# A forgetting-attention layer on one core: transposing the softmax weights on the tensor engine for part of the keys

## The chip, the core and the metric

The kernel runs on one core of one Trainium2 chip. The metric is device time in microseconds (us): the median of three runs, and beside it one execution that the hardware profiler recorded. Engines are named as in the profile: PE is the tensor engine's matmul side and PEld its weight loads, DVE the vector engine, ACT the scalar engine, POOL GpSimd, SP the engine whose queue issues most transfers.

## The reference

One layer of an encoder trunk with 2048 positions and width 1024. The token mixer is causal attention with 16 heads of 64 and a forgetting bias; a dense squared-ReLU MLP follows.

```python
logits = einsum(q_i, k) * scale + (F_i[..., :, None] - F[..., None, :])   # F = cumsum log sigmoid(f_pre + b_f)
logits = where(k_pos[None, :] <= q_pos[:, None], logits, -inf)
p = softmax(logits)
o = einsum(p, v)                     # per block of 128 queries
x = x + g_m * (o @ w_out)
h = rms_norm(x, norm_mlp) * (1 + sc_f) + sh_f
x = x + g_f * (square(relu(h @ w_mlp_in)) @ w_mlp_out)
```

q, k, v come from a normed and modulated x times `fox_w_in`; q and k are RMS-normed per head.

## The kernel before

The program has two parts. The first (0 to about 1,500 us of the profile) holds the attention, the second the MLP.

**Units.** The 16 heads are worked in 8 groups `g` of two heads `h`, and the queries in 16 blocks `i` of 128. A unit is one block of one head: 256 units, of which 128 have `i` of 8 or more, with 1,152 to 2,048 keys. For each unit

- `att_scores` computes the scores on PE (L537, L538, mask L540) into a PSUM tile `S` of up to 1,024 keys; DVE adds the forgetting row and takes the running maximum (L544), writing the scores to the SBUF tile `L`. L549 makes the negative maximum `st`.
- `att_exp` lets ACT take the exponential of all keys in place (L555), and then write, in pieces of up to 1,024 keys (`PW`), the fp16 high half times 32,768 (`PSCALE`) to a tile `ph` (L562).
- `att_transpose` lets DVE write the low half, `L` times 32,768 minus the high half, behind it into the same `ph` (L574). In group 7, for blocks 8 to 15, POOL does the last 256 keys of a piece in two steps (L578 scales, L579 subtracts). Then SP issues a transposing transfer of high and low halves from `ph` to a tile `pT` (L582).
- `att_values` multiplies on PE: per 128 keys one matmul with the high part (L600) and one with the low part (L601), with `pT` as weights, into `po`.

**Buffers.** `L` has 3 buffers (`NL`), `ph` 4 (`NPH`), `pT` 5 (`NPT`). PSUM has two tiles `S`, one bank `T` (`psT`, one buffer, also used when the normed q and k are transposed on PE in `sweep_norm`, L435 and L445), two banks `Q` for the projections and one for `po`.

**Order.** `attention()` is written so that the values of a unit come about three units after its scores. Between them the `sweeps()` generator puts the projections of the next group (L487 to L489, 24 matmuls for 128 positions, with operands split into high and low parts by ACT L406 and POOL L407). The order on each engine's queue is fixed when the program is built, by a list scheduler that works with its own estimates of durations; on the chip each queue runs in that order and waits on semaphores.

**Second part.** The output projection and the MLP, almost all PE (L132 to L134), weights split by ACT L864 and DVE L865.

Of the kernel before, what the change touches and what calls it, by code (L numbers as in the profile page):

```python
# [6 lines left out]

# [17 lines left out]
P = 128  # L25
# [4 lines left out]
HD = 64  # L30
# [9 lines left out]
PSCALE = 32768.0  # L40
PW = 1024
# [10 lines left out]
QSH, QDM = 0, 0  # L52
LEAD0, NORM_AT, ADA0, ADA1, NF = 0.5, 8, 60, 10, 5
# [4 lines left out]
def fox_layer(ctx, tc, x, c, norm_mix, norm_mlp, w_ada, b_ada, w_mlp_in, w_mlp_out,  # L58
# [116 lines left out]
    with ExitStack() as st:  # L175
# [161 lines left out]
        def value_scale(g):  # L337

            wv = sb.tile([P, KB, P], F32, tag="ph" if g else "k", name=f"wv{g}", bufs=NPH if g else NK)
            nc.sync.dma_start(wv, w_in[:, 2 * D + g * P:2 * D + (g + 1) * P].rearrange("(k p) c -> p k c", p=P))  # L340
            r = sb.tile([P, 2], F32, tag="lsr", name=f"lsr_w{g}", bufs=2)
            nc.scalar.activation(wv, wv, AF.Square, accum_out=r[:, 0:1])
            lw = sb.tile([P, 2], F32, tag="lw", name=f"lw{g}", bufs=2)
            log_sum(r, lw, f"w{g}")
            nc.vector.tensor_tensor(lw, lw, hs2, op=ALU.add)
            nc.scalar.activation(vsc[:, g:g + 1], lw[:, 0:1], AF.Exp, scale=-0.5)
            nc.vector.tensor_scalar(vsc[:, g:g + 1], vsc[:, g:g + 1], PSCALE, None, op0=ALU.mult)
            nc.vector.reciprocal(osc[:, g:g + 1], vsc[:, g:g + 1])
            nc.vector.tensor_scalar(osc[:, g:g + 1], osc[:, g:g + 1], 1.0 / PSCALE, None, op0=ALU.mult)

# [171 lines left out]
        def att_scores(g, i, h, st, L):  # L522
# [6 lines left out]
            for cch in range(j + 1):  # L529
# [11 lines left out]
                if last or cch % 2 == 1:  # L541
                    c0, c1 = cch // 2 * 2 * TJ, cch * TJ + w
                    with pri(PR_T):
                        nc.vector.tensor_tensor_reduce(  # L544
                            out=L[:, c0:c1], in0=s2[:, :c1 - c0], in1=Fb[g, h, cch // 2][:, :c1 - c0],
                            scale=1.0, scalar=-3.0e38, op0=ALU.add, op1=ALU.max, accum_out=mx[:, cch // 2:cch // 2 + 1])
                yield
            with pri(PR_T):
                nc.vector.tensor_reduce(out=st[:, h:h + 1], in_=mx[:, :j // 2 + 1], axis=AX.X, op=ALU.max, negate=True)  # L549

        def att_exp(g, i, h, st, L):
# [6 lines left out]
            for s0 in range(0, W, PW):  # L558
                w = min(PW, W - s0)
                ph = sb.tile([P, 2 * PW], F16, tag="ph", name=f"ph{g}_{i}_{h}_{s0}", bufs=NPH)  # L560
                with pri(PR_E):
                    nc.scalar.activation(ph[:, :w], L[:, s0:s0 + w], AF.Copy, scale=PSCALE)  # L562
# [3 lines left out]
        def att_transpose(g, i, h, L, phs):  # L566
            W = (i + 1) * P
            pts = []
            for n, ph in enumerate(phs):
                s0 = n * PW  # L570
                w = min(PW, W - s0)
                c = w - min(w, POOL_B * P) if i >= POOL_I and g >= POOL_G and w > TJ else w
                with pri(PR_PL):
# [9 lines left out]
                pts.append(pT)  # L583
            return pts
# [4 lines left out]
        def att_values(g, i, h, st, pts):  # L589
# [5 lines left out]
            for b in range(nb):  # L595
                v = vT[g, b // RB][:, b % RB, h, :]
                pT, bb = pts[b * P // PW], b % (PW // P)
                nw = min(PW // P, nb - b + bb)
                with pri(PR_PO):
                    nc.tensor.matmul(po[:, h, :], lhsT=pT[:, bb, :], rhs=v, start=(b == 0), stop=False)  # L600
                    nc.tensor.matmul(po[:, h, 0:HD], lhsT=pT[:, nw + bb, :], rhs=v[:, 0:HD],  # L601
# [345 lines left out]
```

## Time and profile before

| what | us |
|---|---|
| median of 3 runs (3115.86 to 3118.42) | 3117.88 |
| profiled execution, its own time | 3121.49 |
| span of that execution | 3119.8 |
| first part, 0 to 1,500 us: PE busy / DVE busy / ACT busy / POOL busy | 1259.7 / 1232.3 / 977.3 / 747.7 |
| second part, 1,500 to 3,120 us: PE busy | 1610.7 |

An engine's busy time is what its instructions cover. Matmuls are pipelined, so PE counts as busy while a matmul drains that no longer hinders the next one. The clock column is the share of full TensorE clock that was granted. "DMA" is the mean busy share of 16 DMA engines; a little over 1.0 means packets that overlap.

### The profile page before, as it was taken

The numbers are of one execution on the slowest core, as the hardware profiler recorded it, in microseconds if no ns is written. First come the engines' busy times: TensorE is split into PE (matmuls) and PEld (weight loads), VectorE is DVE, ScalarE is ACT, GpSimd is POOL, SyncE is SP. The second block draws the span as 40 slices with busy tenths as digits, with TensorE's granted clock in tenths as the row PEclk, the third lists the DMA queues.
The fourth block names the chain that finished last, engine by engine and source line by source line (L and its number), as shares of the span: only waits on it lengthen the run. The fifth ranks groups of instructions, "written<-read, shape, count | busy, mean of one in ns | idle before, by whom it ended". The sixth has DMA issues, their size and how long they took to land.

```text
span 3119.8 us, 44614 instructions
## 1 busy us (share of the span) xinstructions
PE 2870.4 (92%) x16587; PEld 2375.9 (76%) x16587; DVE 1930.7 (62%) x3319; ACT 1433.1 (46%) x2267; POOL 1040.5 (33%) x811
## 2 busy tenths in 40 slices
PE   4788889888988898988999999999999999999999
PEld 4667777777877777776788888788887888878887
DVE  6688978988888877878356433443335333453334
ACT  4466766666676767766233322232222223222321
POOL 3354545545464645445332100410013001311103
PEclk9799989999999999998999999999999999999999
DMA  8479999999999989979755432543235323352332
GB/s 274 124 174 208 208 193 218 209 204 208 213 209 211 201 191 197 189 163 211 215 191 200 132 93 80 172 138 95 75 108 203 94 81 108 95 192 91 108 94 69
DMA packets 852122, 502.34 MB, mean 161 GB/s; under 512 B 585396, under 2 KB 782076, under 8 KB 851904
## 3 DMA queue, kind: packets, MB, share of 16 engines
q1 hardware_dynamic: 843536, 469.60, 62.1%
q0 software_dynamic: 8368, 29.89, 2.5%
q8 instruction: 130, 2.13, 0.3%
q14 instruction: 88, 0.72, 0.1%
HBM read 310.50 MB, written 46.28 MB: 114 GB/s over the span
## 4 chain that ended last, share of the span: by engine, by line
PE 49%; DVE 1%; DMA 1%; ACT 0%; issue 0%; SPq 0%; POOL 0%; DVEq 0%; ACTq 0%
PE my L134 8%; PE my L132 7%; PE my L133 7%; PE pu L134 7%; PE pu L132 7%; PE pu L133 7%; PE py L132 1%; PE py L133 1%; PE py L134 1%; DVE w L865 1%; DMA w1r<-in_w_mlp_in_dram 1%; PE xt L799 0%; PE e_py L132 0%; DMA pT<-ph 0%; PE e_py L134 0%; PE e_py L133 0%
## 5 line engine op out<-in xcount | busy, mean ns | idle before, releaser
L574 DVE SCALAR_TENSOR_TENSOR ph<-L,ph 128x1024 f16<-128x1024 f32 (+7 forms) x384 | 438.3, 1152 | 81.2 <-ACT ph L562 79.5
L887 POOL TENSOR_TENSOR rl<-rl 128x512 f32<-128x512 f32 x128 | 139.1, 1086 | 1024.6 <-ACT rl L886 1019.7
L864 ACT CAST w<-w1r 128x1024 fp32r<-128x1024 f32 x128 | 133.5, 1043 | 598.6 <-PE my L134 553.5
L132 PE MATMUL my<-w,a 128*128 128x512 f32 x1024 | 405.0, 396 | 0.1
L133 PE MATMUL my<-w,a 128*128 128x512 f32 x1024 | 402.9, 394 | 0.0
L134 PE MATMUL my<-w,a 128*128 128x512 f32 x1024 | 395.9, 396 | 2.9 <-DVE a L890 2.9
L562 ACT ACTIVATE ph<-L 128x1024 f16<-128x1024 f32 (+7 forms) x384 | 301.7, 804 | 177.4 <-DMA pT<-ph 152.6
L407 POOL TENSOR_TENSOR hl<-hl,hh 128x1024 fp32r<-128x1024 f32 x120 | 299.5, 2497 | 243.7 <-ACT hh L406 205.4
L487 PE MATMUL psq<-w,hh 128*128 128x384 f32 (+1 forms) x960 | 343.5, 359 | 26.5 <-DVE v L496 12.5
L489 PE MATMUL psq<-w,hl 128*128 128x384 f32 (+1 forms) x960 | 354.4, 371 | 3.2 <-POOL hl L407 2.9
L544 DVE CUSTOM_DVE_ANT_0 L<-S,F 128x1024 f32<-128x1024 f32 (+7 forms) x384 | 343.1, 904 | 19.5 <-PE S L538 6.7
L488 PE MATMUL psq<-w,hh 128*128 128x384 f32 (+1 forms) x960 | 342.7, 359 | 6.1 <-POOL w L333 6.1
L555 ACT ACTIVATE L<-L,st 128x128 f32<-128x128 f32 (+15 forms) x256 | 306.7, 1198 | 89.2 <-DVE st L549 84.9
L537 PE MATMUL S<-kT,qT 128*128 128x512 f32 (+3 forms) x640 | 261.8, 411 | 77.4 <-DVE mx L544 66.6
L600 PE MATMUL po<-v,pT 128*128 128x128 f16 x2176 | 277.1, 228 | 55.4 <-DMA pT<-ph 47.0
L865 DVE TENSOR_TENSOR w<-w1r,w 128x1024 fp32r<-128x1024 f32 x128 | 169.9, 1328 | 236.6 <-ACT w L864 236.6
L915 DVE TENSOR_TENSOR ya<-my,ya 128x512 f32<-128x512 f32 x192 | 128.0, 687 | 292.7 <-PE my L134 292.7
L134 PE MATMUL pu<-m_h,w 128*128 128x512 f32 x768 | 304.4, 396 | 0.0
L132 PE MATMUL pu<-m_h,w 128*128 128x512 f32 x768 | 303.8, 396 | 0.0
L133 PE MATMUL pu<-m_h,w 128*128 128x512 f32 x768 | 301.8, 393 | 0.0
L865 DVE TENSOR_TENSOR w<-w2r,w 128x1024 fp32r<-128x1024 f32 x128 | 165.7, 1295 | 203.7 <-ACT w L864 203.7
L600 PEld LDWEIGHTS <-pT 128*128 128x128 f16 x2176 | 205.1, 103 | 86.2 <-DMA pT<-ph 58.3
(214 smaller groups left out, 6115.8 us busy)
## 6 DMA issues: line engine op xcount, KB each, us to landing
w1r<-in_w_mlp_in_dram SPq DMA_DIRECT2D x128, 512.0 KB
w2r<-in_w_mlp_out_dram SPq DMA_DIRECT2D x128, 512.0 KB
hl<-hT_d SPq DMA_DIRECT2D x120, 512.0 KB
F<-nF_d SPq DMA_DIRECT2D x64, 256.0 KB
wa<-in_w_ada_dram SPq DMA_DIRECT2D x32, 512.0 KB
x<-in_x_dram SPq DMA_DIRECT2D x27, 512.0 KB
wr<-in_fox_w_in_dram SPq DMA_DIRECT2D x64, 192.0 KB
h_d<-h2r POOLq DMA_DIRECT2D x24, 512.0 KB, 3.4
```

What stands on the lines that cost most here:

```text
L132: nc.tensor.matmul(ps, lhsT=a[0], rhs=b[0], start=first, stop=False)
L133: nc.tensor.matmul(ps, lhsT=a[0], rhs=b[1], start=False, stop=False)
L134: nc.tensor.matmul(ps, lhsT=a[1], rhs=b[0], start=False, stop=last)
L487: nc.tensor.matmul(ps[:, :n], lhsT=hh, rhs=w[:, 0, :n], start=(kb == 0), stop=False)
L488: nc.tensor.matmul(ps[:, :n], lhsT=hh, rhs=w[:, 1, :n], start=False, stop=False)
L489: nc.tensor.matmul(ps[:, :n], lhsT=hl, rhs=w[:, 0, :n], start=False, stop=(kb == KB - 1))
L544: nc.vector.tensor_tensor_reduce(out=L[:, c0:c1], in0=s2[:, :c1 - c0], in1=Fb[g, h, cch // 2][:, :c1 - c0], scale=1.0, scalar=-3.0e38, op0 ...
L555: nc.scalar.activation(L[:, :W], L[:, :W], AF.Exp, bias=st[:, h:h + 1], scale=1.0, accum_out=st[:, 2 + h:3 + h])
L562: nc.scalar.activation(ph[:, :w], L[:, s0:s0 + w], AF.Copy, scale=PSCALE)
L574: nc.vector.scalar_tensor_tensor(ph[:, w:w + c], L[:, s0:s0 + c], PSCALE, ph[:, :c], op0=ALU.mult, op1=ALU.subtract)
L600: nc.tensor.matmul(po[:, h, :], lhsT=pT[:, bb, :], rhs=v, start=(b == 0), stop=False)
L865: nc.vector.tensor_tensor(w[:, 1, :], raw, w[:, 0, :].bitcast(F32), op=ALU.subtract)
```

## The change

For blocks 8 to 15 the weights of a unit are cut differently, by the new function `plan(i)`: keys 0 to 511 are transposed by PE, as fp32, into the PSUM bank `T`; ACT copies them to the high half in a `pT` tile and DVE subtracts to make the low half. Keys 512 to 1,023 form a `ph` piece of their own whose low half POOL makes; keys from 1,024 on stay as they were. Blocks 0 to 7 keep their cut. The factor 32,768 moves into the exponential: `st` is the negative maximum plus ln 32,768, so `L` holds scaled weights; L562 becomes a plain copy, L574 a plain subtraction, the scaling step L578 falls away, and the factor in `osc` too. The maximum is chained from the first score tile to the second instead of reduced at the end.

```diff
+TURN_I, HEADS = 8, ("pe", "pool")
@@ value_scale
-            nc.vector.tensor_scalar(osc[:, g:g + 1], osc[:, g:g + 1], 1.0 / PSCALE, None, op0=ALU.mult)
@@ att_scores
-                            scale=1.0, scalar=-3.0e38, op0=ALU.add, op1=ALU.max, accum_out=mx[:, cch // 2:cch // 2 + 1])
+                            scale=1.0, scalar=mx[:, 0:1] if cch > 1 else -3.0e38, op0=ALU.add, op1=ALU.max, accum_out=mx[:, cch // 2:cch // 2 + 1])
-                nc.vector.tensor_reduce(out=st[:, h:h + 1], in_=mx[:, :j // 2 + 1], axis=AX.X, op=ALU.max, negate=True)
+                nc.vector.tensor_scalar(st[:, h:h + 1], mx[:, j // 2:j // 2 + 1], -1.0, LN_PSCALE, op0=ALU.mult, op1=ALU.add)
+
+        def plan(i):
+            W = (i + 1) * P
+            if i < TURN_I:
+                return [(s0, min(PW, W - s0), "dma") for s0 in range(0, W, PW)]
+            head = [(k * TJ, TJ, how) for k, how in enumerate(HEADS)]
+            return head + [(s0, min(PW, W - s0), "dma") for s0 in range(len(head) * TJ, W, PW)]
@@ att_exp
-            for s0 in range(0, W, PW):
-                w = min(PW, W - s0)
+            for s0, w, how in plan(i):
+                if how == "pe":
+                    phs.append(None)
+                    continue
                 ph = sb.tile([P, 2 * PW], F16, tag="ph", name=f"ph{g}_{i}_{h}_{s0}", bufs=NPH)
-                    nc.scalar.activation(ph[:, :w], L[:, s0:s0 + w], AF.Copy, scale=PSCALE)
+                    nc.scalar.copy(ph[:, :w], L[:, s0:s0 + w])
@@ att_transpose
-                    nc.vector.scalar_tensor_tensor(ph[:, w:w + c], L[:, s0:s0 + c], PSCALE, ph[:, :c],
-                                                   op0=ALU.mult, op1=ALU.subtract)
-                    if c < w:
-                        lt = L[:, s0 + c:s0 + w]
-                        nc.gpsimd.tensor_scalar(lt, lt, PSCALE, None, op0=ALU.mult)
-                        nc.gpsimd.tensor_tensor(ph[:, w + c:2 * w], lt, ph[:, c:w], op=ALU.subtract)
+            for (s0, w, how), ph in zip(plan(i), phs):
+                n = w // P
                 pT = sb.tile([P, 2 * PW // P, P], F16, tag="pT", name=f"pT{g}_{i}_{h}_{s0}", bufs=NPT)
-                with pri(PR_DT):
-                    nc.sync.dma_start_transpose(pT[:, :2 * w // P, :], ph[:, :2 * w])
+                if how == "pe":
+                    pt = psT.tile([P, TJ], F32, tag="T", name=f"pp{g}_{i}_{h}")
+                    for b in range(n):
+                        nc.tensor.transpose(pt[:, blk[b]], L[:, s0 + b * P:s0 + (b + 1) * P], ident)
+                    hi, lo = [pT[:, k * n:(k + 1) * n, :].rearrange("p b c -> p (b c)") for k in range(2)]
+                    nc.scalar.copy(hi, pt)
+                    nc.vector.tensor_tensor(lo, pt, hi, op=ALU.subtract)
+                else:
+                    c = w - min(w, POOL_B * P) if i >= POOL_I and g >= POOL_G and w > TJ else w
+                    c = 0 if how == "pool" else c
+                    with pri(PR_PL):
+                        if c > 0:
+                            nc.vector.tensor_tensor(ph[:, w:w + c], L[:, s0:s0 + c], ph[:, :c], op=ALU.subtract)
+                        if c < w:
+                            nc.gpsimd.tensor_tensor(ph[:, w + c:2 * w], L[:, s0 + c:s0 + w], ph[:, c:w], op=ALU.subtract)
+                    with pri(PR_DT):
+                        nc.sync.dma_start_transpose(pT[:, :2 * w // P, :], ph[:, :2 * w])
```

In the changed kernel L587 is the transposing matmul, L589 ACT's copy, L590 DVE's subtraction, L596 DVE's and L598 POOL's subtraction to `ph`, L600 the transposing transfer, L617 and L618 the values (L600 and L601 before).

The PE queue at the values of group 3, block 11, head 1 (`pT3_11_1_0` is the tile with that unit's first keys; `psq` a projection). Before:

```order
L489 MATMUL psq4_1_2_8982<-w4_4_7897,hl4_6_8871 128x384
L487 MATMUL psq4_1_2_8982<-w4_5_7902,hh4_6_8873 128x384
L488 MATMUL psq4_1_2_8982<-w4_5_7902,hh4_6_8873 128x384
L204 MATMUL pvfg_9116<-ident_129,acc4_7032 128x128
L600 LDWEIGHTS pT3_11_1_0_8945
L600 MATMUL po_192<-v3_0_6138,pT3_11_1_0_8945 128x128
```

And in the changed kernel:

```order
L490 MATMUL psq4_3_1_10522<-w4_7_8291,hh4_13_10323 128x384
L491 MATMUL psq4_3_1_10522<-w4_7_8291,hl4_13_10321 128x384
L587 MATMUL pp3_11_1_9380<-ident_129,L3_11_1_9218 128x128 x4
L617 LDWEIGHTS pT3_11_1_0_9379
L617 MATMUL po_192<-v3_0_6390,pT3_11_1_0_9379 128x128
L204 MATMUL pvfg_9575<-ident_129,acc4_7364 128x128 x8
L587 MATMUL pp3_12_0_9469<-ident_129,L3_12_0_9305 128x128 x4
L618 LDWEIGHTS pT3_11_1_0_9379
```

The four transposes now stand directly ahead of the values that read their result, with ACT's copy and DVE's subtraction in between on their own queues.

The SP queue at blocks 12 and 13 of group 3. The last number pair of a row gives the blocks of 128 columns that a transfer turns (high and low halves together). Before:

```order
L582 DMA_TRANSPOSE pT3_12_0_0_9026<-ph3_12_0_0_8951 128x16x128
L582 DMA_TRANSPOSE pT3_12_0_1024_9029<-ph3_12_0_1024_8953 128x10x128
L582 DMA_TRANSPOSE pT3_12_1_0_9105<-ph3_12_1_0_9032 128x16x128
L582 DMA_TRANSPOSE pT3_12_1_1024_9108<-ph3_12_1_1024_9034 128x10x128
L582 DMA_TRANSPOSE pT3_13_0_0_9198<-ph3_13_0_0_9111 128x16x128
L613 DMA o_d11_83<-ot3_11_9191 128x128
```

And in the changed kernel:

```order
L600 DMA_TRANSPOSE pT3_12_0_512_9476<-ph3_12_0_512_9394 128x8x128
L600 DMA_TRANSPOSE pT3_12_0_1024_9479<-ph3_12_0_1024_9396 128x10x128
L630 DMA o_d11_83<-ot3_11_9650 128x128
L600 DMA_TRANSPOSE pT3_12_1_512_9563<-ph3_12_1_512_9483 128x8x128
L600 DMA_TRANSPOSE pT3_12_1_1024_9566<-ph3_12_1_1024_9485 128x10x128
L600 DMA_TRANSPOSE pT3_13_0_512_9664<-ph3_13_0_512_9570 128x8x128
```

As many transfers stand there as before; the first of each unit turns 8 blocks instead of 16.

## Rows read from the trace of the kernel before

**Rows 1.** Stretches: busy time (instructions) per engine, clock, DMA share, GB/s.
```profile
core 0: us, PE busy (x) PEld busy (x) DVE busy (x) ACT busy (x) POOL busy (x), PEclk, DMA share, GB/s
0.00:1500.00 1500.00, 1259.70 (x9519) 1079.12 (x9520) 1232.27 (x2492) 977.33 (x1657) 747.71 (x568) 0.93 0.94 200
1500.00:3120.00 1620.00, 1610.68 (x7069) 1296.80 (x7067) 698.39 (x827) 455.81 (x610) 292.81 (x243) 1.00 0.38 125
```

**Rows 2.** Stretches of blocks 8 to 15, groups 2 to 7.
```profile
545.00:660.00 115.00, 97.99 (x795) 86.23 (x795) 107.50 (x179) 74.88 (x119) 61.49 (x42) 1.00 0.99 204
...
718.00:837.00 119.00, 104.05 (x787) 87.58 (x785) 104.58 (x174) 81.87 (x127) 65.69 (x44) 0.94 1.03 217
...
885.00:1001.00 116.00, 102.60 (x773) 87.09 (x770) 98.97 (x179) 81.89 (x126) 64.85 (x44) 0.94 1.02 213
...
1054.00:1160.00 106.00, 95.18 (x715) 79.73 (x714) 88.74 (x170) 77.35 (x123) 57.78 (x42) 0.97 0.90 191
...
1217.00:1315.00 98.00, 88.84 (x741) 76.76 (x741) 86.95 (x157) 74.47 (x115) 55.64 (x40) 0.97 0.95 190
...
1382.00:1512.00 130.00, 107.03 (x825) 85.94 (x824) 96.30 (x184) 74.20 (x95) 70.45 (x71) 0.89 0.95 195
```

**Rows 3.** Waits, 0 to 1,500 us: engine, line, releaser; total us, times, longest.
```profile
ACT ph L562 <- DMA pT<-ph: 152.6, 103, 6.4
...
DVE ph L574 <- ACT ph L562: 79.5, 78, 3.6
...
PE S L537 <- DVE mx L544: 66.6, 54, 4.7
...
PE po L600 <- DMA pT<-ph: 47.0, 34, 6.5
...
PE psq L487 <- DVE v L496: 12.5, 7, 4.4
```

**Rows 4.** Groups by shape, 0 to 1,500 us: busy, mean ns; idle before them.
```profile
line engine op names shapes xcount | busy us, mean ns | idle before us <-releasers
...
L574 DVE SCALAR_TENSOR_TENSOR ph<-L,ph 128x1024 f16<-128x1024 f32 x142 | 209.8, 1481 | 36.3 <-ACT ph L562 35.3
...
L562 ACT ACTIVATE ph<-L 128x1024 f16<-128x1024 f32 x160 | 168.1, 1055 | 80.1 <-DMA pT<-ph 76.8 <-DVE acc L197 1.9 <-issue 0.4
...
L448 DVE TENSOR_TENSOR kT<-pqk,kT 64x512 fp32r<-64x512 f32 x64 | 44.1, 689 | 11.3 <-ACT kT L447 9.6
...
L578 POOL TENSOR_SCALAR L<-L 128x256 f32<-128x256 f32 x24 | 30.1, 1258 | 40.6 <-ACT ph L562 37.1 <-issue 3.5
...
L579 POOL TENSOR_TENSOR ph<-L,ph 128x256 f16<-128x256 f32 x24 | 20.7, 863 | 1.1
...
L562 ACT ACTIVATE ph<-L 128x512 f16<-128x512 f32 x32 | 19.8, 623 | 6.4 <-DMA pT<-ph 6.3
...
L445 PEld LDWEIGHTS pqk<-ident,qn 128*128 128x128 f32 x128 | 15.5, 147 | 3.7 <-DVE qT L438 1.8 <-issue 1.5
...
L688 POOL TENSOR_TENSOR e_x<-e_x,wo_raw 128x512 f32<-128x512 f32 x3 | 3.9, 1311 | 2.2 <-DVE wo_raw L687 2.2
...
L668 ACT CAST e_oT<-e_pot 128x512 fp32r<-128x512 f32 x6 | 3.3, 581 | 6.5 <-PE e_pot L667 6.5
```

**Rows 5.** Instructions in order of time near 1,000 us: start, us, what.
```profile
1000.83 1.90 POOL L429 TENSOR_TENSOR qn<-qk,y_q 128x1024 f32<-128x1024 f32 x1 [0.25 <-DVE y_q L127]
...
1001.95 1.86 DVE L574 SCALAR_TENSOR_TENSOR ph<-L,ph 128x1024 f16<-128x1024 f32 x1
...
1008.75 1.22 DVE L574 SCALAR_TENSOR_TENSOR ph<-L,ph 128x1024 f16<-128x1024 f32 x1
```

**Rows 6.** Chain of waits near the attention's end: start, us, what.
```profile
1470.12 6.86 DMA pT<-ph
...
1477.09 1.07 ACT ph L562
...
1478.23 1.62 POOL L L578
1479.86 1.46 SPq L582
...
1481.48 4.79 DMA pT<-ph
```

**Rows 7.** The page's DMA packets, by size.
```profile
DMA packets 852122, 502.34 MB, mean 161 GB/s; under 512 B 585396, under 2 KB 782076, under 8 KB 851904
```

More of the change, by code (lines that the diff above doesn't have):

```diff
@@ L8 @@
+import math
 from contextlib import ExitStack
@@ L40 @@
 PSCALE = 32768.0
+LN_PSCALE = math.log(PSCALE)
 PW = 1024
@@ L566, in att_transpose @@
         def att_transpose(g, i, h, L, phs):
[L567 to L573, printed above, removed]
-                    nc.vector.scalar_tensor_tensor(ph[:, w:w + c], L[:, s0:s0 + c], PSCALE, ph[:, :c],
-                                                   op0=ALU.mult, op1=ALU.subtract)
-                    if c < w:
-                        lt = L[:, s0 + c:s0 + w]
-                        nc.gpsimd.tensor_scalar(lt, lt, PSCALE, None, op0=ALU.mult)
-                        nc.gpsimd.tensor_tensor(ph[:, w + c:2 * w], lt, ph[:, c:w], op=ALU.subtract)
-                pT = sb.tile([P, 2 * PW // P, P], F16, tag="pT", name=f"pT{g}_{i}_{h}_{s0}", bufs=NPT)
-                with pri(PR_DT):
-                    nc.sync.dma_start_transpose(pT[:, :2 * w // P, :], ph[:, :2 * w])
-                pts.append(pT)
@@ L584, in att_transpose @@
-            return pts
+            by_block = []
+            for (s0, w, how), ph in zip(plan(i), phs):
+                n = w // P
+                pT = sb.tile([P, 2 * PW // P, P], F16, tag="pT", name=f"pT{g}_{i}_{h}_{s0}", bufs=NPT)
+                if how == "pe":
[15 more added lines that the diff above has]
+                        nc.sync.dma_start_transpose(pT[:, :2 * w // P, :], ph[:, :2 * w])
+                by_block += [(pT[:, b, :], pT[:, n + b, :]) for b in range(n)]
@@ L586, in fox_layer @@
+            return by_block
         po_of, n_po = {}, [0]
@@ L596, in att_values @@
                 v = vT[g, b // RB][:, b % RB, h, :]
-                pT, bb = pts[b * P // PW], b % (PW // P)
-                nw = min(PW // P, nb - b + bb)
+                p_hi, p_lo = pts[b]
                 with pri(PR_PO):
-                    nc.tensor.matmul(po[:, h, :], lhsT=pT[:, bb, :], rhs=v, start=(b == 0), stop=False)
-                    nc.tensor.matmul(po[:, h, 0:HD], lhsT=pT[:, nw + bb, :], rhs=v[:, 0:HD],
+                    nc.tensor.matmul(po[:, h, :], lhsT=p_hi, rhs=v, start=(b == 0), stop=False)
+                    nc.tensor.matmul(po[:, h, 0:HD], lhsT=p_lo, rhs=v[:, 0:HD],
                                      start=False, stop=(b == nb - 1))
```

## The prediction
> **What bounds the kernel now.** I read the stretches first. After 1,500 us PE is busy 1,610.7 of 1,620 us [rows 1]; the change touches nothing there, so that part keeps its length. All that can move lies in the first 1,500 us, where no engine is full: PE 1,259.7, DVE 1,232.3, ACT 977.3, and the DMA engines at 0.94 [rows 1]. The reader is to see there that PE is idle for 240 us, and that three resources are each close to their limit at once. The changed blocks are read in stretches of their own, from the first scores of block 8 to the first scores of the next group [rows 2]. For groups 2 to 6 these last 115, 119, 116, 106 and 98 us, 554 in all. In them DVE is busy 486.7 us (88%), PE 488.6 us (88%), and the DMA share is 0.90 to 1.03. PEld, the weight loads, whose ends are not modelled as those of the matmuls are, stands at 417.4 us (75%), so PE has more room than its own row says.
>
> Next the waits [rows 3]. PE waits 66.6 us for a score tile that DVE has not yet drained, 47.0 us for a transposed tile, 12.5 us for a projection bank that DVE has not drained. ACT waits 152.6 us for a `ph` tile whose transfer hasn't left, and DVE 79.5 us for ACT behind that. So the transfers hold up ACT, ACT holds up DVE, and DVE holds up PE; but PE pays only 126 us for all three waits named. That is the most that the change can give back on PE, against what it puts on PE.
>
> **The change, part by part.**
>
> PE gets 128 units x 4 = 512 transposes of 128x128 fp32. The same operation stands in the trace: its weight load takes 147 ns [rows 4], which is what a run of them advances by, so 512 x 0.147 = 75 us of PE time, 9.4 us in each group's stretch. No PE work goes away. PE is idle 12% of such a stretch, and as many of the transposes may fall into idle time: **+66 us** (bounds 0, all in idle time, and 75).
>
> New round trips on PE's queue. Values of keys 0 to 511 wait for ACT's copy (0.58 us) and DVE's subtraction (0.69 us) of what PE has just transposed [rows 4]: 1.27 us at least when nothing stands between. In the order on PE's queue 23 of the 128 units have at most 8 matmuls between the last transpose and the first values matmul (15 have none), the other 105 have 23 or more. And bank `T` has one buffer: 14 of the transposes follow those of the unit before by 13 matmuls or fewer, so they wait for the same two steps. (23 + 14) x 1.27 = 47 us if PE had nothing late at those places before; zero if it would have idled there anyway. I take half: **+24 us**. If ACT has an exponential of 2,048 keys ahead of the copy, it is more, and that is in the upper end.
>
> The ring of `pT`. A unit takes three of the five tiles instead of two. Before, the transfer of keys from 1,024 on waits for values of two units earlier; now for the values of keys 0 to 511 of the unit just before (so in the program: the third piece of block 12, head 1, waits for the first piece of block 12, head 0). Release, issue (1.46 us) and landing (4.79 to 6.86 us for 2,048 columns [rows 6]) must now fit into about one unit, and a unit of these blocks lasts 554 us / 80 = 6.9 us. Before they had two. Behind the waiting issue on SP stand the next group's `hl` loads and the output store. On the other side a unit's first transfer turns 1,024 columns instead of 2,048, and over all 128 x 1,024 = 131,072 columns of 256 B leave the DMA queue. The program before turns 557,056 columns, most of the 585,396 packets under 512 B [rows 7], so 24% of them go. Two effects on PE's 47.0 us: down to nothing at best (-47), and at worst a mean wait of 47.0 / 34 = 1.38 us in each of the 128 units (+177 - 47 = +130). The shorter transfer and the tighter ring nearly balance; I take **+10 us**.
>
> DVE loses the 1,024-key subtraction, 1,481 ns [rows 4], and gets one of 512 keys out of PSUM, 689 ns for the nearest row (64 partitions, same length): 128 x 0.79 = 101 us less, 12.7 us per stretch, from 88% to about 77%. The chained maximum and the changed L549 swap one short instruction for another: nothing. What PE can gain from it are the waits on DVE, 66.6 + 12.5 = 79 us; with DVE at 77% I take 70%: **-55 us** (bounds 0 and -79; -101 if DVE alone set the pace).
>
> Of the 1,481 ns part is a collision: at 1001.95 the subtraction took 1.86 us beside a POOL instruction, at 1008.75 it took 1.22 us without one [rows 5]. The new subtraction reads one operand from PSUM, POOL's new one reads two from SBUF. The Trainium skill (SBUF, "Who interferes with whom") says that a vector instruction with two SBUF inputs and a GpSimd instruction that reads SBUF exclude each other, and one with a single SBUF input is free. The two rows agree. By that rule POOL's added time would fall on the subtractions that DVE keeps and give back some 30 of the 101 us; the sum would be about 15 us higher.
>
> POOL gets 128 subtractions of 512 keys. The nearest rows are 863 ns for 256 keys of the same kind and 1,311 ns for 512 of fp32 [rows 4]: 1.3 us each (up to 1.7), 166 us on an engine with 752 us free, less the 30.1 us of L578. It is hidden by that idle time. What loses if the cover goes is the split of the projection's operand queued behind it. ACT does two copies of 512 keys instead of one of 1,024: 2 x 0.62 - 1.06 = 0.19 us x 128 = 24 us, hidden, with 523 us free.
>
> The end of the attention. Group 7 has no projections left to fill with, and its stretch lasts 130 us instead of 111. The chain there runs through a transfer of 6.86 us, L578 with 1.62 us and a transfer of 4.79 us [rows 6]. L578 goes, and the first transfer of each unit halves: **-10 us** (bounds 0 and -19).
>
> Sum: 66 + 24 + 10 - 55 - 10 = **+35 us**. The profiled execution took 3,121.49 us with a span of 3,119.8, 3.6 above the median of 3,117.88; on the median 3,117.9 + 35 = **3,153 us**.
>
> **The rivals.**
>
> A, the relief is worth more than PE's new work: **faster**. For it: DVE and DMA are as full as PE in these stretches, and PEld shows room: (417.4 + 5 x 9.4) / 554 = 84%. If the first part is paced by DVE, its 101 us come off; against that stands that PE can't go beyond 97 to 100% busy. Price: the waits of PE on DVE and transfers nearly all go (-126), the tail gives -19, the transposes cost 75 and no new wait shows: -70, or 3,048 us; with half the new round trips 3,060. I put it at 3,060. It decides from the point at which PE's idle time in the first part falls from 240 to under 165 us. The Trainium skill (VectorE: DVE Perf Modes, "The three transpose paths") points this way: for a full 128x128 it advises the tensor engine where PSUM can take the result, with 390 ns there against 1,309 ns by DMA. No row here shows that latency for a single block; 4.79 us for 16 blocks is 0.30 us each, and 147 ns the load on PE.
>
> B, both sides cancel within 6 us: 3,118 us. For it: the terms are of one size, +100 and -65.
>
> C, the ring decides: the third piece lands late in most units. 1.46 + 4.79 us and the queue on SP against a unit of 6.9 us leave 0.65 us. Price: half of the +130, in place of the +10: 3,208 us; with ACT's queue ahead of the copies up to 3,240. For it: ACT already waits 152.6 us for transfers. Against it: the first piece is half as long, and a landing only counts from the ninth block of the unit on.
>
> That the change doesn't do what it says is excluded by the order: the 512 transposes stand on PE, and the transfers are halved.
>
> **How the numbers follow.** My forecast (slower by some 35 us) 0.38, A 0.36, B 0.12, C 0.14. A difference of 0.2%, 6 us, is about what a measurement here can tell from none. Faster 0.36, within 0.2% 0.12, slower 0.52. Since A and the forecast hold most and have different signs, the forecast's own range is 3,130 to 3,190; the whole range reaches from A's 3,060 less a little to C's: 3,055 to 3,230.
>
> **What would show it.** Right: PE busy in 0 to 1,500 us up by 50 to 75 us; L590 near 0.69 us on 128 instructions; waits of `S` on L546 well below 66.6 us; new waits of L617 and L618 on ACT and DVE of 20 to 50 us, and of L587 on DVE; waits for transposed tiles near 50 us, with the DMA share down by a fifth. Wrong for A: PE idle in the first part below 165 us. Wrong for C: waits of L617 on DMA above 100 us. A second part that isn't 1,610 us long would break the ground of all of this.

## The result

The changed kernel takes 3,270.24 us (median of four runs, 3,261.76 to 3,275.01) beside 3,118.15 us for the kernel before: a ratio of 1.0486, 95% interval 1.046 to 1.0512, or 152 us more. Forecast were 35 us more, with 3,230 us as the upper end. The profiled execution took 3,274.3 us with a span of 3,272.6.

The page of the changed kernel: busy time and share of the span of each engine, and the DMA packets.

```profile
PE 2945.1 (90%) x17099; PEld 2467.0 (75%) x17099; DVE 1851.5 (57%) x3311; ACT 1446.9 (44%) x2395; POOL 1130.5 (35%) x899
...
DMA packets 721057, 468.88 MB, mean 143 GB/s; under 512 B 454324, under 2 KB 651004, under 8 KB 720832
```

The packets under 512 B fell by 131,072 [rows 7], exactly one for each turned column that left the queue. The two parts of the changed kernel, cut where its last 1,623 us begin, in the columns of [rows 1]:

```profile
0.00:1650.00 1650.00, 1336.91 (x10053) 1171.49 (x10054) 1155.43 (x2487) 992.23 (x1787) 840.55 (x661) 0.90 0.72 162
1650.00:3273.00 1623.00, 1608.23 (x7048) 1295.52 (x7046) 696.07 (x824) 454.70 (x608) 289.94 (x239) 1.00 0.39 124
```

The second part is what it was, so all of the loss lies in the attention. There, in 1,650 us instead of 1,500, DVE's busy time fell by 77 us and the DMA share from 0.94 to 0.72, as the change means it to. But PE is busy 77 us longer (1,336.9 against 1,259.7), idle 313 us instead of 240, and its granted clock fell from 0.93 to 0.90 [rows 1].

The waits of that first part, in the columns of [rows 3] (`plsw` is a small matmul that also writes bank `T`):

```profile
POOL ph L598 <- ACT ph L574: 237.2, 88, 11.9
...
ACT ph L574 <- DMA pT<-ph: 134.6, 85, 6.0
...
PE S L539 <- DVE mx L546: 66.4, 68, 5.0
...
PE po L617 <- DMA pT<-ph: 48.5, 37, 6.0
...
DVE L L546 <- PE pp L587: 41.8, 31, 2.4
...
PE pp L587 <- DVE kT L450: 36.5, 12, 4.5
...
PE pqk L447 <- DVE qT L440: 29.1, 8, 7.3
...
PE psq L489 <- DVE v L498: 20.8, 10, 3.7
...
PE plsw L233 <- DVE lsr_w L231: 15.9, 6, 3.5
...
PE po L617 <- ACT pT L589: 14.0, 20, 1.6
```

Three kinds are to be told apart. The wait of `S` on DVE, most of which the change was to take away, is 66.4 us where it was 66.6 [rows 3]. The wait for transposed tiles is 48.5 us where it was 47.0. And there is a kind that hardly existed before: PE's transposes of the weights (L587) and the two transposes of the projection (L437, L447) take turns in bank `T` and wait for DVE, which reads it, 36.5 + 29.1 = 66 us; DVE in its turn waits 41.8 us for PE's transposes before it may write a score buffer. The 15.9 us of `plsw` are another thing: L231 writes that matmul's own input, so there PE waits for a late DVE and not for the bank. Before the change the corresponding rows were:

```profile
PE pqk L445 <- DVE qT L438: 2.8, 3, 1.3
...
PE plsw L230 <- DVE lsr_w L228: 1.8, 2, 1.6
```

The groups by shape of the changed kernel, in the columns of [rows 4]:

```profile
L598 POOL TENSOR_TENSOR ph<-L,ph 128x512 f16<-128x512 f32 x128 | 156.9, 1225 | 234.2 <-ACT ph L574 233.1 <-DVE v_q L124 0.7
...
L587 PE MATMUL pp<-ident,L 128*128 128x128 f32 x512 | 92.4, 310 | 43.6 <-DVE kT L450 36.5 <-DVE st L551 2.6 <-DVE lw L234 1.5
L590 DVE TENSOR_TENSOR pT<-pp,pT 128x512 f16<-128x512 f32 x128 | 87.4, 683 | 9.4 <-ACT pT L589 7.6
L589 ACT CAST pT<-pp 128x512 f16<-128x512 f32 x128 | 74.2, 580 | 58.1 <-PE pp L587 57.5 <-PE po L618 0.3
L587 PEld LDWEIGHTS pp<-ident,L 128*128 128x128 f32 x512 | 68.8, 159 | 57.0 <-issue 43.5 <-DVE st L551 2.8 <-DVE gate L225 2.4
```

Each new operation lasts about what the prediction took for it. What went wrong must lie between the operations.

**One round trip.** Rows in order of time in group 3 of the changed kernel (start, us, what):

```profile
1046.19 0.60 PE L587 MATMUL pp<-ident,L 128*128 128x128 f32 x4
...
1047.05 1.47 ACT L565 ACTIVATE L<-L,st 128x1408 f32<-128x1408 f32 x1 [1.98 <-DVE st L551]
...
1048.52 1.03 ACT L408 CAST hh<-hl 128x1024 fp32r<-128x1024 f32 x1
1049.45 0.36 ACT L496 COPY qk<-psq 128x256 f32<-128x256 f32 x1
...
1049.71 0.37 ACT L497 ACTIVATE v<-psq,vsc 128x128 f16<-128x128 f32 x1
1049.98 0.58 ACT L589 CAST pT<-pp 128x512 f16<-128x512 f32 x1
...
1050.59 0.69 DVE L590 TENSOR_TENSOR pT<-pp,pT 128x512 f16<-128x512 f32 x1
```

The four transposes are done at 1,046.79 and bank `T` is free at 1,051.28: 4.5 us, of which the copy and the subtraction are 1.27. Ahead of the copy ACT worked off an exponential, a split and two copies of the projection. Over all 128 units the trace gives, from the last transpose's end, 0.97 us until ACT begins, 0.58 for the copy, 0.94 until DVE begins and 0.68 for the subtraction: 3.17 us, two and a half times the 1.27 us of the prediction.

**Who else uses the bank.** Rows of group 1, where the projections turn q and k in the same bank:

```profile
734.70 1.06 PE L437 MATMUL pqk<-ident,qn 128*128 128x128 f32 x4
...
739.77 0.76 DVE L440 SCALAR_TENSOR_TENSOR qT<-pqk,qgain,qT 64x512 fp32r<-64x512 f32 x1
740.64 0.71 PEld L447 LDWEIGHTS pqk<-ident,qn 128*128 128x128 f32 x4 [3.36 <-issue]
740.67 1.08 PE L447 MATMUL pqk<-ident,qn 128*128 128x128 f32 x4 [3.24 <-DVE qT L440]
...
744.57 1.09 PE L587 MATMUL pp<-ident,L 128*128 128x128 f32 x4 [2.82 <-DVE kT L450]
```

PE stands still for 3.24 and for 2.82 us. The first of these waits lies between the projection's own two transposes, which shared the bank before the change as well; what is new there is that DVE comes to them later. The second is that of the weights for the bank. PE also turns slowly: four transposes take 1.06 to 1.09 us here, against 0.60 in the fence before. The granted clock goes with it: here is an earlier stretch in which PE was nearly always busy, and the stretch of these rows (columns as in [rows 1]):

```profile
709.00:717.00 8.00, 7.01 (x77) 6.10 (x75) 7.38 (x17) 4.42 (x7) 4.75 (x3) 0.97 0.74 143
734.00:747.00 13.00, 5.89 (x44) 4.24 (x43) 8.03 (x13) 5.89 (x8) 6.83 (x7) 0.63 0.57 142
```

PE was busy 5.89 of 13 us in the second stretch, and its clock was mostly at the lower of its two levels (1.2 of 2.4 GHz); in the first it was busy 7.01 of 8 us and almost always at the higher one. In the second stretch PE's waits went with slower matmuls, so they may have cost twice, once as idle time and once in what ran behind them; no run separates the two.

### The profile page after: what moved, and what is told of

It reads as the page before. It is cut to its first block, busy times and chain, and to the rows that moved or that the text cites. A ratio compares the mean times of both kernels' runs of the same rounds, so it can differ in the third digit from the quotient of the medians.

```text
span 3272.6 us, 46131 instructions
## 1 busy us (share of the span) xinstructions
PE 2945.1 (90%) x17099; PEld 2467.0 (75%) x17099; DVE 1851.5 (57%) x3311; ACT 1446.9 (44%) x2395; POOL 1130.5 (35%) x899
## 4 chain that ended last, share of the span: by engine, by line
PE 48%; DMA 2%; DVE 1%; ACT 0%; issue 0%; SPq 0%; DVEq 0%; ACTq 0%
PE my L137 7%; PE my L135 7%; PE my L136 7%; PE pu L137 7%; PE pu L135 7%; PE pu L136 7%; PE py L135 1%; PE py L136 1%; PE py L137 1%; DVE w L882 1%; DMA w1r<-in_w_mlp_in_dram 1%; DMA pT<-ph 1%; PE e_py L135 0%; PE e_py L136 0%; PE e_py L137 0%; PE xt L816 0%
## 5 line engine op out<-in xcount | busy, mean ns | idle before, releaser
L565 ACT ACTIVATE L<-L,st 128x128 f32<-128x128 f32 (+15 forms) x256 | 307.7, 1202 | 124.9 <-DVE st L551 120.6
L489 PE MATMUL psq<-w,hh 128*128 128x384 f32 (+1 forms) x960 | 339.1, 355 | 26.3 <-DVE v L498 20.8
L409 POOL TENSOR_TENSOR hl<-hl,hh 128x1024 fp32r<-128x1024 f32 x120 | 291.7, 2433 | 177.4 <-ACT hh L408 144.2
L491 PE MATMUL psq<-w,hl 128*128 128x384 f32 (+1 forms) x960 | 338.5, 355 | 0.0
L539 PE MATMUL S<-kT,qT 128*128 128x512 f32 (+3 forms) x640 | 272.5, 426 | 71.2 <-DVE mx L546 66.4
L490 PE MATMUL psq<-w,hh 128*128 128x384 f32 (+1 forms) x960 | 334.1, 351 | 0.0
L617 PE MATMUL po<-v,pT 128*128 128x128 f16 x2176 | 263.4, 231 | 73.3 <-DMA pT<-ph 55.0
L574 ACT CAST ph<-L 128x512 f16<-128x512 f32 (+7 forms) x384 | 244.4, 651 | 170.0 <-DMA pT<-ph 134.6
L596 DVE TENSOR_TENSOR ph<-L,ph 128x128 f16<-128x128 f32 (+7 forms) x256 | 255.1, 1000 | 88.7 <-ACT ph L574 87.4
L546 DVE CUSTOM_DVE_ANT_0 L<-S,F 128x1024 f32<-128x1024 f32 (+7 forms) x256 | 250.9, 984 | 69.9 <-PE pp L587 41.8
L617 PEld LDWEIGHTS <-pT 128*128 128x128 f16 x2176 | 209.1, 105 | 106.6 <-DMA pT<-ph 62.6
```

The lines of the kernel that those rows point to most:

```text
L409: nc.gpsimd.tensor_tensor(hl, hl.bitcast(F32), hh.bitcast(F32), op=ALU.subtract)
L489: nc.tensor.matmul(ps[:, :n], lhsT=hh, rhs=w[:, 0, :n], start=(kb == 0), stop=False)
L490: nc.tensor.matmul(ps[:, :n], lhsT=hh, rhs=w[:, 1, :n], start=False, stop=False)
L491: nc.tensor.matmul(ps[:, :n], lhsT=hl, rhs=w[:, 0, :n], start=False, stop=(kb == KB - 1))
L539: nc.tensor.matmul(sp, lhsT=q[:, h, qs], rhs=k[:, h, :w], start=True, stop=False)
L565: nc.scalar.activation(L[:, :W], L[:, :W], AF.Exp, bias=st[:, h:h + 1], scale=1.0, accum_out=st[:, 2 + h:3 + h])
```

## The experiments

Each time is set against the kernel before on the same chip; a difference in us is the ratio less one, times 3,118 us. The changed kernel stands at +152 us. The compiler's scheduler orders every kernel anew, so a run changes small things besides its edit.

### The single parts without PE

`bias_only`, the scale in the exponential's bias alone, with the cut and the transfers as before:

```diff
-TURN_I, HEADS = 8, ("pe", "pool")
+TURN_I, HEADS = 16, ("pe", "pool")
```

> Only the scale in the exponential's bias, the plain copy and subtraction that follow from it, and the chained maximum; the cut of before for all blocks, nothing on PE, POOL as before less L578. My reading (nothing): 3,105 to 3,125 us. Rival (the chained maximum makes DVE's second score tile wait for the accumulator of the first, 0.1 us on 128 units and more behind them): 3,130 us or more.

Measured: 3,120.28 us, ratio 1.0004 (0.9992 to 1.0017). The bias costs and gives nothing, as priced.

`pool_half`: as `bias_only`, and POOL makes the low part of keys 512 to 1,023 inside the undivided first piece.

```diff
...
-                    c = 0 if how == "pool" else c
+                    c = TJ if i >= 8 and s0 == 0 else c
```

> As bias_only, but POOL makes the low part of keys 512 to 1,023 in blocks 8 to 15 inside the first piece of 1,024 keys; no new piece, no third pT tile, nothing on PE. Theory P (POOL's 128 subtractions of 1.2 us cost, since the transfer and the operand splits wait for them): at least 30 of the 44 us that no_pe lost, 3,150 us or more. Theory R (the third piece costs): 3,090 to 3,125 us, since DVE has 75 us less to do.

Measured: 3,125.25 us, ratio 1.0023 (1.0013 to 1.0033), +7 us. So handing this work from DVE to POOL brings nothing by itself. DVE loses little by it: its subtractions of half as many keys take 1,027 ns on average where those of 1,024 keys took 1,512 in `bias_only`, and its busy time in the first part falls from 1,249 us there to 1,230.

`cut_only`: three pieces and three `pT` tiles per unit, all turned by transfers, and DVE makes the low parts of the first 1,024 keys.

```diff
-TURN_I, HEADS = 8, ("pe", "pool")
+TURN_I, HEADS = 8, ("dma", "dma")
```

> As no_pe, but DVE also makes the low part of keys 512 to 1,023: the first 1,024 keys cut into two pieces with transfers of their own, three pT tiles per unit, POOL and PE as before. Theory R: as slow as no_pe or slower, 3,155 to 3,190 us. Theory P: near before, 3,115 to 3,135 us.

Measured: 3,153.46 us, ratio 1.0113 (1.0092 to 1.0133), +35 us. The waits of ACT for a `ph` tile and of PE for a transposed tile in the first 1,533 us (152.6 and 47.0 us before [rows 3]):

```profile
ACT ph L574 <- DMA pT<-ph: 192.9, 165, 4.8
...
PE po L617 <- DMA pT<-ph: 82.3, 71, 5.7
```

PE waits 71 times for transposed tiles instead of 34, and as many us longer as the kernel is slower. But this cut is tighter than that of the changed kernel: a unit takes three of the five `pT` tiles in both, but here also three of the four `ph` tiles and three transfers, where the changed kernel keeps two of each. In the changed kernel PE's wait for tiles is 48.5 us and ACT's 134.6. So the 35 us are the price of this cut, and how much of them is the ring of `pT`, for which the prediction had +10, isn't shown.

`no_pe`: the new cut with POOL's part, but the first 512 keys turned by a transfer.

```diff
-TURN_I, HEADS = 8, ("pe", "pool")
+TURN_I, HEADS = 8, ("dma", "pool")
```

> The changed cut and scale, but keys 0 to 511 of blocks 8 to 15 go by ACT copy, DVE subtraction and a transposing transfer of their own (three transfers per unit, three of five tiles), so PE turns nothing; POOL still makes the low part of keys 512 to 1,023. Theories T and W (the loss comes from PE's transposes and their bank): near the kernel before, 3,100 to 3,150 us. Theory R: still slow, 3,200 us or more. A theory that POOL's part costs (its 128 subtractions hold up the operand splits): 3,170 or more.

Measured: 3,162.35 us, ratio 1.0133 (1.0117 to 1.0149), +41 us: about the 35 us of the cut and the 7 of POOL's part together. So PE's transposes, which were to bring the gain, make the kernel 110 us slower than transfers in the same cut. The Trainium skill (VectorE: DVE Perf Modes, "Rules for kernel authors") advises the tensor engine for a transpose of 128x128 where PSUM can take the result. For this kernel the measurement decides against it; the advice doesn't weigh who waits for the bank.

### What PE's transposes cost

The next three kernels build up from nothing to the change, one reason for waiting at a time.

`no_turn`: no transposes; ACT and DVE make both parts straight from the score buffer.

```diff
-                    pt = psT.tile([P, TJ], F32, tag="T", name=f"pp{g}_{i}_{h}")
-                    for b in range(n):
-                        nc.tensor.transpose(pt[:, blk[b]], L[:, s0 + b * P:s0 + (b + 1) * P], ident)
+                    pt = L[:, s0:s0 + TJ]
```

> The changed kernel with the 512 transposes left out: ACT's copy and DVE's subtraction of keys 0 to 511 read the weights in L directly, so the values are computed with untransposed weights. Everything else stays (three pT tiles, POOL's part, the copies). If PE's transposes with their bank and what hangs on them cost the 108 us between no_pe and the changed kernel: 3,140 to 3,165 us. If the copies into pT, queued on ACT and DVE behind the ring, cost as well: 3,190 us or more.

Measured: 3,080.35 us, ratio 0.9888 (0.9853 to 0.9923), -35 us. This is all of the change but PE's part, with three `pT` tiles and two transfers per unit as in the changed kernel, so whatever the ring costs is in it. Half of the first transfer is gone, POOL makes a part, and together that brings 35 us. DVE's subtractions take 408 us here (281.2 + 127.0) where they took 438.3 on the page before, so its relief is small.

`turn_unread`: `no_turn` and 512 transposes of a constant into bank `T`, which nobody reads.

```diff
-                        nc.tensor.transpose(pt[:, blk[b]], L[:, s0 + b * P:s0 + (b + 1) * P], ident)
+                        nc.tensor.transpose(pt[:, blk[b]], ones128, ident)
+                    pt = L[:, s0:s0 + TJ]
```

> The 512 transposes are made of a constant, and nobody reads what they write: ScalarE and VectorE make the high and low parts of keys 0 to 511 straight from the unturned score buffer, as in no_turn. So the turn of those keys is left out of the result. The step over no_turn (3080 us) is the price of TensorE's own time alone, with no wait on either side. Theory O (own time): 512 x 147 ns = 75 us, less what falls in its idle time: 3140 to 3155. Theory W (waits: the score buffer held, bank T held until both parts are read) expects the same here, and the rest of the 190 us in the next run. Rival: the transposes fall into TensorE's 250 us of idle time, and nearly all of the 190 us is waits: 3085 to 3115.

Measured: 3,112.11 us, ratio 0.9975 (0.9964 to 0.9985), -8 us. PE's own time for the transposes costs 27 us, and with that alone the change would be slightly faster than before. A constant is ready at any time, so the scheduler was free to put these transposes where PE idled; 27 us is the price in such places.

`turn_unread_l`: the transposes read the score buffer again; what they write is still not read.

```diff
+                    pt = L[:, s0:s0 + TJ]
```

> As turn_unread, but the transposes read the score buffer, so that they wait for the exponential and hold the buffer until they are done; what they write is still read by nobody (ScalarE and VectorE read the unturned buffer). The step over turn_unread is the price of that wait and hold, and the step from here to the changed kernel (3270 us) is that of bank T being held until both parts have been read, and of the parts waiting for TensorE. From turn_const (24 us below the changed kernel without the hold): +15 to +35 over turn_unread. If the bank is what counts, this run lies at 3165 to 3190 and the last step is 80 to 105 us; if the hold is, at 3200 to 3260.

Measured: 3,179.35 us, ratio 1.0189 (1.0171 to 1.0208), +59 us. Waiting for the exponential and holding the score buffer, with the place in PE's queue that follows from it, cost 67 us. The waits that name them directly, those between L587 and the exponential (L565) and between L546 and L587, are small in the first 1,556 us; the other two rows are waits on the bank:

```profile
PE pp L587 <- DVE kT L450: 9.5, 8, 2.8
...
DVE L L546 <- PE pp L587: 9.1, 12, 1.8
...
PE pp L587 <- ACT L L565: 5.6, 6, 1.3
PE pqk L447 <- DVE qT L440: 5.6, 4, 2.2
```

By which waits the rest of the 67 us comes about isn't shown. From here to the changed kernel, where ACT and DVE read bank `T` and hold it meanwhile, are another 93. In this step the two waits on the bank grow from 9.5 + 5.6 to 36.5 + 29.1 us, by 51 us.

The first parts of the three, cut 1,620 us from the end, in the columns of [rows 1]; `no_turn`:

```profile
0.00:1456.00 1456.00, 1226.48 (x9539) 1069.42 (x9540) 1209.85 (x2484) 985.73 (x1785) 861.35 (x656) 0.94 0.82 184
```

`turn_unread`:

```profile
0.00:1490.00 1490.00, 1273.97 (x10026) 1102.78 (x10027) 1232.29 (x2484) 987.17 (x1785) 856.62 (x658) 0.96 0.82 179
```

`turn_unread_l`:

```profile
0.00:1556.00 1556.00, 1305.35 (x10026) 1135.08 (x10027) 1210.76 (x2484) 989.32 (x1785) 852.26 (x658) 0.93 0.76 172
```

From `turn_unread` to the changed kernel PE executes the same instructions (some 30 of them fall on the other side of the cut). Its idle time goes from 216 over 251 to 313 us, +97, and its busy time from 1,274 over 1,305 to 1,337 us, +63, while its clock goes from 0.96 over 0.93 to 0.90. These two are the 160 us by which the part grew. In the last step alone PE's idle time grows by 62 us, and the 51 us of the bank are most of that. In `no_turn`, `turn_unread` and `turn_unread_l` DVE's subtraction reads SBUF and takes longer than the changed kernel's 683 ns:

```profile
L591 DVE TENSOR_TENSOR pT<-L,pT 128x512 f16<-128x512 f32 x128 | 138.3, 1081 | 17.5 <-ACT pT L590 17.1
```

(this row is of `turn_unread`). The changed kernel is spared that, so the last step, the bank's, is rather more than 93 us than less.

`turn_const` takes the hold away from the whole change: a constant is turned, ACT and DVE read the bank.

```diff
-                        nc.tensor.transpose(pt[:, blk[b]], L[:, s0 + b * P:s0 + (b + 1) * P], ident)
+                        nc.tensor.transpose(pt[:, blk[b]], ones128, ident)
```

> The changed kernel, but the 512 transposes read a constant tile instead of the weights, so they wait for no exponential and, above all, a score buffer L is free without them (the values of keys 0 to 511 are then those of a constant). Theory L (three score buffers, each held until PE has turned it; DVE's L546 waits 41.8 us for that, and PE's scores behind it): 25 to 50 us come back, 3,220 to 3,245 us, with no wait of L546 for the transposes. Without theory L: within 12 us of 3,270.

Measured: 3,245.76 us, ratio 1.0416 (1.0386 to 1.0445), 22 us less than the changed kernel, not 67. Taken in this order, the bank with its readers costs 138 us over `turn_unread` and the hold 22 on top; in the other order they were 93 and 67. Their sum of 160 us is measured, and its split depends on the order, since the two overlap. A likely reading is that while PE waits for the bank, waiting for the score buffer is partly free.

`turn_twice`: each transpose is issued twice.

```diff
-                    for b in range(n):
+                    for b in list(range(n)) * 2:
```

> The changed kernel with each of the 512 transposes done twice into the same place: 512 more on PE, nothing else. Theory W (PE sets the pace of the first part): +75 us at full clock up to +95, 3,345 to 3,365 us. Theories T and R (PE waits for others there): much of it falls into waits, +20 to +50 us, 3,290 to 3,320.

Measured: 3,309.97 us, ratio 1.0611 (1.0595 to 1.0626), 39 us more than the changed kernel. 512 further transposes of 147 ns cost half of their 75 us here, and the first 512 cost a third in `turn_unread`: work alone isn't the 187 us between `no_turn` and the change.

### Taking the waits away

`pqk_in_q`: the projection's transposes go to the two banks `Q`; `T` is left to the weights.

```diff
-            pt = psT.tile([P, TJ], F32, tag="T", name=f"pqk{g}_{j}_0")
+            pt = psQ.tile([P, TJ], F32, tag="Q", name=f"pqk{g}_{j}_0")
...
-            pt = psT.tile([P, TJ], F32, tag="T", name=f"pqk{g}_{j}_2")
+            pt = psQ.tile([P, TJ], F32, tag="Q", name=f"pqk{g}_{j}_2")
```

> The changed kernel, but the normed q and k of the projections are transposed into the two Q banks, so bank T belongs to the weights' transposes alone. Theory T (the shared bank: in the changed kernel PE idles 36.5 us before the weights' transposes for DVE L450 and 29.1 us before those of k for DVE L440, against 2.8 us before): 60 to 90 us come back, some 3,180 to 3,210 us. Theory W (what costs is the transposes' own 75 us of PE time and the slower clock): within 15 us of the changed kernel's 3,270. Theory R (three tiles of a ring of five): within 15 us of 3,270 too.

Measured: 3,223.63 us, ratio 1.0339 (1.0322 to 1.0357), 46 us less than the changed kernel. What is left of these waits in its first 1,604 us (the last row now concerns a bank `Q`):

```profile
PE pp L587 <- DVE pT L590: 9.0, 12, 1.3
...
PE pp L587 <- DVE lw L234: 2.1, 2, 1.0
...
PE pqk L447 <- DVE qT L440: 1.1, 1, 1.1
```

The 36.5 and 29.1 us are gone. What the prediction had counted on this bank, a unit's transposes behind those of the unit before, is the 9.0 us row. The 46 us were the price of the shared use. The round trip itself didn't get shorter: over the 128 units of this trace it takes 3.93 us on average, against 3.17 in the changed kernel. Its length matters by what stands behind it.

`own_ring`: the part that PE turns gets two small tiles of its own, and the ring `pT` four for two pieces (one start-up load moves to another buffer for that).

```diff
-NL, NPH, NPT, NK, NV, NQD = 3, 4, 5, 6, 7, 1
+NL, NPH, NPT, NK, NV, NQD = 3, 4, 4, 6, 7, 1
...
+                own = how == "pe"
-                pT = sb.tile([P, 2 * PW // P, P], F16, tag="pT", name=f"pT{g}_{i}_{h}_{s0}", bufs=NPT)
+                pT = sb.tile([P, (PW if own else 2 * PW) // P, P], F16, tag="pS" if own else "pT", name=f"pT{g}_{i}_{h}_{s0}", bufs=2 if own else NPT)
```

> The changed kernel, but the tiles with keys 0 to 511 have a ring of their own (two of half size), and the transposing transfers keep four of full size, so a unit waits for values two units back again (one start-up load goes to another buffer for that). Theory R (the ring of five with three per unit): 40 to 80 us come back, 3,190 to 3,230 us, and PE's waits for transposed tiles fall from 48.5 us to under 25. Theories T and W: within 20 us of 3,270 us.

Measured: 3,240.27 us, ratio 1.0385 (1.0367 to 1.0403), 32 us less. The wait for transposed tiles fell to 22.1 us, and that on `pqk` rose to 37.2.

`own_ring_q` has both edits.

```diff
-            pt = psT.tile([P, TJ], F32, tag="T", name=f"pqk{g}_{j}_0")
+            pt = psQ.tile([P, TJ], F32, tag="Q", name=f"pqk{g}_{j}_0")
...
+                own = how == "pe"
...
```

> own_ring and pqk_in_q together: both the ring and the bank relieved. If the bank's 47 us and the ring's 30 us are separate, 3,190 to 3,200 us; if the two stand for the same waits, 3,215 to 3,230. What is left above 3,118 us is then the transposes' own time on PE, some 40 us by turn_twice, and what no_pe lost.

Measured: 3,221.39 us, ratio 1.0335 (1.031 to 1.036), 47 us less, hardly more than `pqk_in_q` alone. The two waits overlap.

`turn_early` gives the transposes the priority of the scores.

```diff
-                        nc.tensor.transpose(pt[:, blk[b]], L[:, s0 + b * P:s0 + (b + 1) * P], ident)
+                        with pri(PR_S):
+                            nc.tensor.transpose(pt[:, blk[b]], L[:, s0 + b * P:s0 + (b + 1) * P], ident)
```

> The changed kernel with the transposes given the scheduler's priority of the scores. If the place of the transposes in PE's queue is a choice of the scheduler, they move ahead, L comes free sooner, and 20 to 40 us come back: 3,230 to 3,250 us. If their place is set by the bank T and the ring behind it, the order hardly changes: 3,260 to 3,280 us.

Measured: 3,250.58 us, ratio 1.0423 (1.0384 to 1.0462), 20 us less.

`one_tile_q_early` joins `turn_early` and `pqk_in_q`, and keys 0 to 1,023 share one `pT` tile.

```diff
...
-                pT = sb.tile([P, 2 * PW // P, P], F16, tag="pT", name=f"pT{g}_{i}_{h}_{s0}", bufs=NPT)
+                if i < TURN_I or s0 != TJ:
+                    both = sb.tile([P, 2 * PW // P, P], F16, tag="pT", name=f"pT{g}_{i}_{h}_{s0}", bufs=NPT)
+                pT = both[:, 8:16, :] if i >= TURN_I and s0 == TJ else both
...
```

> All reliefs at once: keys 0 to 1,023 share one pT tile again (two tiles of five per unit, as before the change), the projections' q and k are transposed in the Q banks, and the transposes have the scores' priority. If ring, bank and held L make up all but PE's own time: 3,118 + 40 to 75 = 3,160 to 3,195 us. If one of them stands in for another: 3,205 to 3,225, like own_ring_q.

Measured: 3,195.5 us, ratio 1.0256 (1.0222 to 1.0289): half of the loss is back, and it stays slower than the kernel before.

### Versions that might beat the kernel before

`last_group`: the change in group 7 alone, where no projection needs bank `T`, with one `pT` tile for keys 0 to 1,023.

```diff
-            if i < TURN_I:
+            if i < TURN_I or g < NG - 1:
...
```

> The changed way only in group 7 (of 8), where no projection of q and k is left that uses bank T, and with one pT tile for the two pieces of keys 0 to 1023; groups 0 to 6 as before. If bank T and the third pT tile are what the change pays for, then the last group keeps most of the relief without them: 64 transposes are 64 x 147 ns = 9 us, an eighth of the relief of no_turn is 5 us and the end of the attention 10 us earlier: 3103 to 3120. If the turns cost the same 0.37 us each wherever they stand (190 us / 512), then 3130 to 3140.

Measured: 3,120.11 us, ratio 0.9997 (0.9988 to 1.0007).

`pool_last`: the bias as changed, and POOL's half in group 7 alone.

```diff
...
-                    c = 0 if how == "pool" else c
+                    c = TJ if i >= 8 and s0 == 0 and g == NG - 1 else c
```

> The scale in the exponential's bias everywhere, no transposes on TensorE, three pieces and pT tiles as before; GpSimd takes the low part of keys 512 to 1023 in group 7 alone. In pool_half (GpSimd's part in all groups, +5 us) the stretch of group 7 was 119 us where it was 130 before. If that holds without the other groups' delay: 3105 to 3115, 3 to 13 us below before. If the 11 us were only work moved across the stretch's border: 3116 to 3124.

Measured: 3,120.83 us, ratio 1.001 (0.9997 to 1.0022). Neither differs from the kernel before by more than can be measured. No full version beats it.

## Why the prediction was wrong

**The step that failed** is "new round trips on PE's queue", +24 us. The runs put 160 us on them: the wait for the exponential with the held score buffer, and the bank, 67 and 93 us in one order of taking them away, 22 and 138 in the other. With 27 us for PE's own time and -35 for the rest this is the measured +152. Three things were wrong in the step. The round trip was taken as 1.27 us, when nothing stands between; it is 3.17 us on average, and the rows show other work of ACT's queue ahead of the copy. The 14 places counted for bank `T` were transposes behind transposes, when the bank is also used by the projection's, which were named in the description of the buffers and not in the sum; `pqk_in_q` shows these at 46 us. And nothing was put down for the score buffer: before, ACT and DVE, which fill it, were also its readers (with POOL in group 7); now PE's transposes are among them, and DVE waits 41.8 us for them.

**PE's own time**, +66, was too high: 27 us in `turn_unread`. From `no_turn` to `turn_unread` PE's busy time rose by 47 us instead of 75, while its mean clock went from 0.94 to 0.96, and its idle time fell by 13 us.

**The relief and the ring**, -55 - 10 + 10 = -55 together, measured -35 in `no_turn`. What of this is the ring stays open: `cut_only` has a tighter cut, and the 32 us that `own_ring` gives back vanish beside the bank's relief (`own_ring_q`). That the sum comes within 20 us is in part luck, since the wait on DVE from which most of the -55 was to come didn't fall in `no_turn`, as the next paragraph shows.

**DVE's relief never reached PE.** In the changed kernel DVE's subtractions took 343 us (255.1 + 87.4) instead of 438.3, 96 us less and near the forecast 101, and still the wait of `S` on DVE stood at 66.4 us. That DVE now waits for PE's transposes can't be the whole reason, for the wait is no shorter where DVE waits for none. The first parts of `no_turn`, `turn_unread` and `pool_half`, one row each:

```profile
PE S L539 <- DVE mx L546: 77.2, 70, 4.1
...
PE S L539 <- DVE mx L546: 70.5, 69, 4.1
...
PE S L539 <- DVE mx L546: 92.0, 80, 4.5
```

The prediction turned a lower busy share of DVE, 77%, into 70% of this wait; no run shows a fall of that size. What sets the wait stays open. The 35 us of `no_turn` came in another place: against the kernel before, PE's first part is 33 us shorter in busy time (1,226.5 against 1,259.7, its clock at 0.94 against 0.93) and 11 us in idle time.

**The rule on SBUF.** The prediction cites the Trainium skill (SBUF, "Who interferes with whom") for some 30 us by which POOL's work would lengthen the subtractions that DVE keeps. Those of 1,024 keys took 1,600 ns in `no_turn` and 1,307 in the changed kernel, against 1,481 before [rows 4] in another form of instruction and 1,512 in `bias_only` in the same form. The few rows that are left of this size are not all of the same blocks. In the full change the price doesn't show.

**The signs.** Right: L590 at 683 ns on 128 instructions, the wait for transposed tiles near 50 us, the DMA share, L587's wait for DVE, the second part. Wrong: the wait of `S`. PE's busy time up by 77 us was forecast as 50 to 75 and came out for another reason: it is the same instructions at a lower clock as much as the transposes, since `turn_unread`, with all 512, is at 1,274 us against 1,259.7 before. Waits of L617 on ACT were 14 us instead of 20 to 50. Rival A asked for PE idle below 165 us; it was 313. Rival C came nearest in size, by luck, for another cause: its sign, over 100 us of waits for transfers, stood at 48.5.

**What stays open.** No run tells what of the bank's 93 to 138 us is PE's wait for its readers and what the readers' wait for PE, none shows by which waits the held score buffer costs its 22 to 67 us, and none keeps the clock up while PE waits. The best version with all 512 transposes, `one_tile_q_early`, is still 80 us slower than the kernel before. That the 63 us of longer busy time are the clock's is read from the rows, not tested.

## What to carry to other kernels

An operation moved to another engine costs its duration, most of which was hidden here, and the waits around its round trip, which were not: price the trip with what stands ahead in the readers' queues, two and a half to three times their own durations here, and ask what stands behind it. List every user of the buffer that the new operation writes, and for every buffer that it reads ask who freed it before and who frees it now. An experiment that issues the work and lets nobody read it parts the two prices in one run. Where two waits overlap, take them away in both orders before calling a share the price of either.

## What the runs showed of the hardware

With 512 fp32 transposes of 128x128 added, unread and reading a constant, the mean granted clock of the first part was 0.96, and 0.94 without. The same matmuls, some 10,030, kept PE busy 1,274 us at a mean clock of 0.96 and 1,337 us at 0.90. In a stretch where PE was busy 5.89 of 13 us the clock was 0.63, and four transposes took 1.08 us instead of 0.60.
